# Attention values in the free quarter of the projection's PSUM bank, at the unit's end

## The chip, the cores and the metric

The kernel runs on one core of one Trainium2 chip. The metric is the device time of the program in microseconds; a run's time is compared with that of the kernel before. Engines are named as in the profile: PE is TensorE's matmul and PEld its weight load, DVE is VectorE, ACT is ScalarE, POOL is GpSimd, SP issues the transfers.

## The reference

One layer of retention, then one layer of differential attention, over 1024 tokens of width 1024. What matters here is the second layer, with 8 heads; each head has two query and key parts of 64 columns and values of 128 columns:

```python
kv = rmsnorm(x, kv_norm) @ w_kv            # keys (rotated) and values
proj = h @ w_in_b                          # queries (rotated) and gate
# for each head and each block of 128 queries, keys up to the block's end:
sc = einsum('bqhtd,bkhtd->bhtqk', q_i, kf) * scale
p = softmax(where(mask, sc, neg))          # for both parts t
w = p[:, :, 0] - lam * p[:, :, 1]
o = einsum('bhqk,bkhe->bqhe', w, vf)
o = rmsnorm(o, sub_norm_b) * (1 - lambda_init)
y = (o * silu(gate)) @ w_out_b
```

## The kernel before

All products of activations with weights are made three times, from a high and a low part of each operand (`mm3`, L95 to L100; the parts are made by `split`, L85 to L92, the high one by ScalarE, the low one by VectorE). The retention layer, its output projection and the gate of the second layer come first and aren't touched. The stage that is changed lies between about 949 and 1405 us.

In it a loop runs over 64 units, 8 heads times 8 token blocks of 128. A unit projects one token block for one head: eight slabs of 128 rows, three matmuls each, into 384 columns of one PSUM bank (`pq`: 256 columns of q and k, 128 of v). After the last slab `rotate_b` applies the rotary embedding: two products on VectorE out of the bank (L501, L502), their sum on GpSimd (L503), and the copy of v by ScalarE (L504). In the next unit `transpose_b` turns the 128 rows of q and k on TensorE (L512) and splits them (L87 on ScalarE, L88 on VectorE).

Between the slabs, two units behind (`LAG = 2`), the attention of one query block is done in pieces, which the generator `attend` hands out:

- `scores`: the two score products (L526; 6 matmuls for blocks 0 to 3, 12 for blocks 4 to 7), VectorE's mask and maximum (L532, L533), ScalarE's exponentials (L534), VectorE's combination of both softmaxes into one weight tile (L536 to L539).
- `turn`: the weight tile is transposed on TensorE, at most four blocks of 128 keys at a time (L551), and copied to wT by ScalarE (L552). Blocks 4 to 7 need two such pieces.
- `values`: the product of wT with v (L562; the trace has two instructions for each block of keys), the copy out of PSUM with a scale (L565), a sum of squares (L566), the power on GpSimd (L105 on VectorE, L106), the normed output (L568) and its store to `og2d` (L569).

In step j of `attend` the pieces are `scores` of block j, `values` of block j-2, and `turn` of block j-1; they run behind slabs 1, 3, 5 and 7. `transpose_b` runs behind slab 4.

PSUM has three groups of buffers: "g", two of one bank (the projection's `pq` among them), "s2", two of two banks (the scores), and "s", two of one bank. Before the change four things of a unit use "s": the transposes of q and k, both `turn` pieces, and the product of `values`.

`ahead` loads and splits the next head's weights (L90, L91), in the trace in the last unit of a head and the first of the next. After the loop `attend` still has steps to give; between their pieces the output projection runs (`out_prep`, which multiplies by the gate at L600 and transposes, and `out_gemm`), three groups of matmuls behind each piece.

The program is written in this order, but the framework lays out the order of every engine by its own estimate of when operands are ready, and sets all waits. It is seen in the trace: in most units TensorE's order is that of the program, in some, several projection matmuls stand ahead of a transpose.

Of the kernel before, what the change touches and what calls it, by code (L numbers as in the profile page):

```python
# [18 lines left out]
P = 128  # L19
# [16 lines left out]
def yoco_kernel(ctx: ExitStack, tc: tile.TileContext, a: dict):  # L36
# [16 lines left out]
    def sbuf(tag, shape, dt, nm):  # L53
        return sb.tile(shape, dt, name=f"{nm}_{next(uid)}", tag=tag, bufs=BUFS[tag])

    def xt(shape, nm, dt=F32R):
        return sbuf("x", shape, dt, nm)

    def wt(shape, nm, dt=F32R):
        return sbuf("w", shape, dt, nm)  # L60
# [7 lines left out]
    def kt(shape, nm, dt=F32):  # L68
        return sbuf("k", shape, dt, nm)

    def sm(n):
        return sbuf("m", [P, n], F32, "m")
# [3 lines left out]
    def ps(tag, n=512):  # L76
        return psum.tile([P, n], F32, name=f"p{tag}_{next(uid)}", tag=tag, bufs=PB[tag])
# [17 lines left out]
    def mm3(out, ops, first=True, last=True):  # L95
        n = 3 * len(ops)
        i = 0
        for lh, ll, rh, rl in ops:
            for l, r in ((lh, rh), (lh, rl), (ll, rh)):
                nc.tensor.matmul(out, l, r, start=(first and i == 0), stop=(last and i == n - 1))  # L100
                i += 1

    def rsqrt(out, in_, mul, add, n=1):
        t = sm(n)
        nc.vector.tensor_scalar(out=t, in0=in_, scalar1=mul, scalar2=add, op0=ALU.mult, op1=ALU.add)  # L105
        nc.gpsimd.tensor_tensor(out=out, in0=t, in1=mhalf[:, 0:n], op=ALU.pow)  # L106
# [166 lines left out]
    prev = None  # L273
    early = [ps("g"), ps("g")]
    gemm_qkv(list(enumerate(early)), w_next[0], range(NS))
    for i in range(H * NC):
        h, c = divmod(i, NC)
        if c == 0:
            wq, wg = w_next
        u = {"h": h, "c": c, "wg": wg, "pp": ps("s2", 1024)}  # L280
# [11 lines left out]
        prev = u  # L292
# [138 lines left out]
    def x2s(c, s):  # L431
        th, o = c // 4, (c % 4) * P
        return x2T[th][0][:, s, o : o + P], x2T[th][1][:, s, o : o + P]

    def gemm_piece(pq, w, c, s):
        mm3(pq, [(*x2s(c, s), w[s][:, 0, :], w[s][:, 1, :])], s == 0, s == NS - 1)
# [10 lines left out]
    def ahead(w, c, s):  # L447

        if s == 0 and 1 <= c <= 4:
            slab(w, c - 1)  # L450
        if c == NC - 1 and s < 4:
            slab(w, 4 + s)
# [21 lines left out]
    w_cur, w_next = w_next, []  # L474
    gate_unit(0, 0)
    fin1(NC - 1)
    for u in range(1, 2 * NC):
        if u == NC:
            w_cur, w_next = w_next, []
# [13 lines left out]
    def rotate_b(h, c, pq):  # L493

        qk, v = group(h, c)
        r = rot
        x4 = pq[:, 0:256].rearrange("p (x e d) -> p x e d", x=4, e=2)
        o4 = lambda t: t.rearrange("p (x e d) -> p x e d", x=4, e=2)
        cb = cosB[:, c, :].unsqueeze(1).unsqueeze(1).to_broadcast([P, 4, 2, 32])
        snb = ssinB[:, c].unsqueeze(1).to_broadcast([P, 4, 2, 32])  # L500
        nc.vector.tensor_tensor(out=o4(r[:, 0]), in0=x4, in1=cb, op=ALU.mult)  # L501
        nc.vector.tensor_tensor(out=o4(r[:, 1]), in0=x4[:, :, ::-1], in1=snb, op=ALU.mult)  # L502
        nc.gpsimd.tensor_tensor(out=r[:, 2], in0=r[:, 0], in1=r[:, 1], op=ALU.add)  # L503
        nc.scalar.activation(v[:, c % 4], pq[:, 256:384], AF.Copy)  # L504
        return h, c, r

    def transpose_b(h, c, r):
        qk, v = group(h, c)
        o = (c % 4) * P
        pt = ps("s", 256)  # L510
        for i in range(2):
            nc.tensor.transpose(pt[:, i * P : (i + 1) * P], r[:, 2, i * P : (i + 1) * P], ident)  # L512
        pv = pt.rearrange("p (x k) -> p x k", x=2)
        split(qk[:, :, 0, o : o + P], qk[:, :, 1, o : o + P], pv)

    def scores(u):
        h, b, nk = u["h"], u["b"], u["nk"]
        q, qs = groups[h, b // 4][0][:, 0], slice(b % 4 * P, b % 4 * P + P)
        sc = [ps("s2", 1024) for t in range(2)]
        for c0 in range(0, nk, 512):  # L520
            n = min(512, nk - c0)
            k = groups[h, c0 // 512][0][:, 1]
            for i, (ql, kl) in enumerate(((0, 0), (0, 1), (1, 0))):
                for t in range(2):
                    rows = slice(t * 64, t * 64 + 64)
                    nc.tensor.matmul(  # L526
                        sc[t][:, c0 : c0 + n], q[rows, ql, qs], k[rows, kl, 0:n], start=(i == 0), stop=(i == 2)
                    )
        nm, s_ = sm(2), sm(2)
        pr = [kt([P, D], f"pr{t}") for t in range(2)]  # L530
        for t in range(2):
            nc.vector.memset(sc[t][0:64, nk - 64 : nk], NEG)  # L532
            nc.vector.tensor_reduce(out=nm[:, t : t + 1], in_=sc[t][:, :nk], axis=AX.X, op=ALU.max, negate=True)  # L533
            nc.scalar.activation(pr[t][:, :nk], sc[t][:, :nk], AF.Exp, bias=nm[:, t : t + 1], accum_out=s_[:, t : t + 1])  # L534
        rc, cf = sm(2), sm(1)
        nc.vector.reciprocal(rc, s_)  # L536
        nc.vector.tensor_scalar(out=cf, in0=s_[:, 0:1], scalar1=rc[:, 1:2], scalar2=nlam, op0=ALU.mult, op1=ALU.mult)
        w = pr[0][:, :nk]
        nc.vector.scalar_tensor_tensor(out=w, in0=pr[1][:, :nk], scalar=cf, in1=w, op0=ALU.mult, op1=ALU.add)  # L539
        u.update(w=w, rc=rc)  # L540

    def turn(u, i):
        w = u["w"]
        if i == 0:
            u["wT"] = kt([P, D], "wT")
        k0, k1 = i * 512, min(u["nk"], i * 512 + 512)
        if k0 >= k1:
            return
        pt = ps("s")
        for k in range(k0, k1, P):  # L550
            nc.tensor.transpose(pt[:, k - k0 : k - k0 + P], w[:, k : k + P], ident)  # L551
        nc.scalar.activation(u["wT"][:, k0:k1], pt[:, : k1 - k0], AF.Copy)  # L552

    valued = set()

    def values(u):
        h, b, wT, rc = u["h"], u["b"], u["wT"], u["rc"]
        valued.add((h, b))
        po = ps("s", P)
        for kb in range(b + 1):  # L560
            v = groups[h, kb // 4][1]
            nc.tensor.matmul(po, wT[:, kb * P : (kb + 1) * P], v[:, kb % 4], start=(kb == 0), stop=(kb == b))  # L562
        o = sbuf("u", [P, 2, P], F32, "o")
        sq, r = sm(1), sm(1)
        nc.scalar.activation(o[:, 0], po, AF.Copy, scale=rc[:, 0:1])  # L565
        nc.scalar.activation(o[:, 1], o[:, 0], AF.Square, accum_out=sq)  # L566
        rsqrt(r, sq, 1.0 / P, EPS)
        nc.gpsimd.tensor_tensor(out=o[:, 1], in0=o[:, 0], in1=r.to_broadcast([P, P]), op=ALU.mult)  # L568
        nc.sync.dma_start(og2d[b * P : (b + 1) * P, h * P : (h + 1) * P], o[:, 1])  # L569

    def attend(blocks):

        blocks = [{"h": h, "b": b, "nk": (b + 1) * P} for h, b in blocks]
        a_, b_ = None, None
        for u in blocks + [None, None]:
            pieces = []
            if u:
                pieces.append(lambda: scores(u))
            if a_:
                pieces.append(lambda: values(a_))  # L580
            if b_:
                pieces.append(lambda: turn(b_, 0))
                if b_["nk"] > 512:
                    pieces.append(lambda: turn(b_, 1))
            yield pieces
            a_, b_ = b_, u


    wob = {}
# [1 line left out]
    def load_wob(f, hi, lo):  # L591
        wob[f] = load_wo(a["wob"], f, gsub, hi, lo)
# [46 lines left out]

    LAG = 2  # L640
    att = attend([(h, b) for h in range(H) for b in range(NC)])
    prev = None
    for i in range(H * NC):
        h, c = divmod(i, NC)
        if c == 0:
            w_cur, w_next = w_next, []
        pieces = next(att) if i >= LAG else []
        pq = ps("g", 384)
        for s in range(NS):
            gemm_piece(pq, w_cur, c, s)  # L650
            ahead(h + 3, c, s)
            if s == 4 and prev:
                transpose_b(*prev)
            if s % 2 == 1 and s // 2 < len(pieces):
                pieces[s // 2]()
        prev = rotate_b(h, c, pq)
        if h == H - 1:
            if c == 4:
                xw = [xt([P, 4, D], f"wob{hl}") for hl in range(2)]
            if 1 <= c <= 2:  # L660
                load_wob(c + 3, wt([P, D], "wobh"), wt([P, D], "wobl"))
            elif c >= 4:
                load_wob(c - 4, xw[0][:, c - 4], xw[1][:, c - 4])
# [4 lines left out]
    out_prep(0)  # L668
    og_ = outs()
    for step in att:  # L670
        for p in step:
            p()
            for _ in range(3):
                next(og_, None)
# [86 lines left out]
```

## Time and profile before

| | us |
|---|---|
| median of 3 runs | 1524.19 (1524.13 to 1524.55) |
| the profiled execution | 1519.59 |
| its span, first to last instruction | 1517.8 |
| TensorE busy in the span | 1480.0 |
| VectorE, ScalarE, GpSimd busy | 782.9, 626.3, 266.2 |

The granted TensorE clock was 0.997 of full speed over the span. A row of a timeline has the start, the duration of a run of like instructions, engine, line, operation, tiles, shapes, the count, and in brackets the idle time of the engine before it with what ended it. A row of waits has the engine and its line, whom it waited for, and the total, the count and the longest. A row of busy times by stretch has the stretch, its length, and the busy time (and count) of PE, PEld, DVE, ACT and POOL, the clock, the share of the transfer engines and GB/s.

### The profile page before, as it was taken

Reading aid. Unit: us, or ns where it says so; the run is one execution under the profiler, and the core shown is the slowest. Engines: PE = TensorE matmul, PEld = TensorE weight load, DVE = VectorE, ACT = ScalarE, POOL = GpSimd, SP = SyncE. Lnnn points to the kernel's source line nnn. Section 1 sums busy time; section 2 is a strip of 40 time slices with the busy share of each in tenths; the row PEclk is TensorE's granted clock in tenths of the full one; section 3 lists DMA queues with packets and bytes.
Section 4 is the critical chain, followed back from the end, with each engine's and each line's share of the span. In section 5 each row is a group of like instructions: output and inputs, shape, how many; then the busy total and the mean of one; then the engine's idle time right before and its main releaser. Section 6 shows DMA issues by size and latency. Waiting matters only on the chain.

```text
span 1517.8 us, 23752 instructions
## 1 busy us (share of the span) xinstructions
PE 1480.0 (98%) x8752; PEld 1296.0 (85%) x8752; DVE 782.9 (52%) x1968; ACT 626.3 (41%) x1591; POOL 266.2 (18%) x470
## 2 busy tenths in 40 slices
PE   6999999999999999999999999999999999999998
PEld 5888998888889888888877788988988988987786
DVE  5664645454545443541145511667567577577543
ACT  5542424242424232342244522456455466465421
POOL 1322222212222222200000000222222222222100
PEclk9999999999999999999999999999999999999999
DMA  7430302021211210353244522111011011023352
GB/s 272 146 111 15 97 15 88 22 82 31 60 53 47 62 62 30 98 191 104 98 153 167 190 95 71 34 47 52 10 51 51 11 51 51 12 92 115 116 174 84
DMA packets 70308, 125.63 MB, mean 83 GB/s; under 512 B 7600, under 2 KB 40752, under 8 KB 70192
## 3 DMA queue, kind: packets, MB, share of 16 engines
q1 hardware_dynamic: 70192, 124.11, 25.2%
q8 instruction: 69, 1.13, 0.3%
q14 instruction: 47, 0.39, 0.1%
HBM read 94.72 MB, written 29.36 MB: 82 GB/s over the span
## 4 chain that ended last, share of the span: by engine, by line
PE 80%; DVE 6%; DMA 5%; ACT 4%; issue 4%; POOL 1%; SPq 0%; DVEq 0%; POOLq 0%; ACTq 0%
PE pg L100 54%; PE ps L100 14%; PE ps L526 3%; PE ps L562 3%; PE ps L551 2%; DMA stg<-in_wa 1%; ACT pr L534 1%; DMA stw<-in_wa 1%; PE ps L313 1%; DVE wbh L91 1%; PE ps L234 1%; DMA og<-ogd 1%; PE ps L512 1%; DMA xr<-in_x 1%; DVE m L533 1%
## 5 line engine op out<-in xcount | busy, mean ns | idle before, releaser
L100 PE MATMUL pg<-wq,xT 128*128 128x512 f32 x1536 | 387.6, 402 | 8.8 <-ACT wq L90 7.1
L100 PEld LDWEIGHTS pg<-wq,xT 128*128 128x128 f32 x1536 | 281.5, 190 | 65.0 <-ACT wq L90 7.1
L100 PE MATMUL pg<-wbh,x2T 128*128 128x384 f32 x1536 | 334.6, 353 | 0.0
L100 PEld LDWEIGHTS pg<-wbh,x2T 128*128 128x128 f32 x1536 | 256.4, 189 | 13.0 <-issue 9.3
L106 POOL TENSOR_TENSOR m<-m,mhalf 128x1 f32<-128x1 f32 x152 | 83.3, 548 | 652.8 <-DVE m L105 591.2
L100 PE MATMUL ps<-wg,xT 128*128 128x256 f32 x1536 | 194.8, 283 | 0.0
L100 PEld LDWEIGHTS ps<-wg,xT 128*128 128x128 f32 x1536 | 189.1, 192 | 0.1
L534 ACT ACTIVATE pr<-ps,m 128x256 f32<-128x256 f32 (+7 forms) x128 | 94.0, 737 | 92.1 <-DVE m L533 92.1
L209 POOL TENSOR_TENSOR a<-a 128x256 f32<-128x256 f32 x64 | 48.1, 752 | 340.4 <-DVE a L208 324.9
L533 DVE TENSOR_REDUCE m<-ps 128x1 f32<-128x256 f32 (+7 forms) x128 | 91.1, 753 | 0.0
L100 PE MATMUL pg<-wbg,x2T 128*128 128x512 f32 x384 | 87.9, 390 | 0.8 <-DVE wbg L91 0.8
L90 ACT ACTIVATE r<-pg,tabA 128x256 fp32r<-128x256 f32 x64 | 30.1, 470 | 136.7 <-DVE a L208 136.2
L100 PEld LDWEIGHTS pg<-wbg,x2T 128*128 128x128 f32 x384 | 71.8, 188 | 16.0 <-DVE wbg L91 1.2
L100 PEld LDWEIGHTS ps<-r,r 128*128 128x128 f32 x528 | 72.1, 190 | 8.6 <-ACT r L236 2.6
L235 DVE TENSOR_TENSOR a<-ps,tabA 128x128 f32<-128x128 f32 x64 | 18.5, 289 | 116.5 <-PE ps L234 116.5
L100 PE MATMUL ps<-r,r 128*128 128x256 f32 x528 | 74.8, 283 | 2.4 <-ACT r L236 2.0
L562 PE MATMUL ps<-v,wT 128*128 128x128 f32 x576 | 74.7, 275 | 0.0
L562 PEld LDWEIGHTS ps<-v,wT 128*128 128x128 f32 x576 | 73.2, 191 | 0.7 <-DVE m L105 0.4
L503 POOL TENSOR_TENSOR tabB<-tabB 128x256 f32<-128x256 f32 x64 | 48.5, 758 | 127.9 <-DVE tabB L502 127.6
L207 DVE TENSOR_TENSOR a<-pg,tabA 128x256 f32<-128x256 f32 x64 | 27.0, 423 | 80.6 <-PE pg L100 80.5
L236 ACT ACTIVATE r<-a 128x128 fp32r<-128x128 f32 x64 | 19.8, 309 | 111.6 <-DVE a L235 111.5
L100 PE MATMUL pg<-wo,oh 128*128 128x512 f32 x192 | 59.9, 391 | 0.0
(142 smaller groups left out, 2344.0 us busy)
## 6 DMA issues: line engine op xcount, KB each, us to landing
stw<-in_wa SPq DMA_DIRECT2D x64, 256.0 KB, 3.0
stb<-in_wbh SPq DMA_DIRECT2D x64, 192.0 KB, 2.4
xr<-in_x SPq DMA_DIRECT2D x16, 512.0 KB, 4.2
stg<-in_wa SPq DMA_DIRECT2D x32, 256.0 KB, 3.3
ogd<-a SPq DMA_DIRECT2D x64, 128.0 KB, 1.9
sto<-in_woa SPq DMA_DIRECT2D x16, 512.0 KB, 4.8
og<-ogd SPq DMA_DIRECT2D x16, 512.0 KB, 5.0
y0d<-y SPq DMA_DIRECT2D x8, 512.0 KB, 3.2
```

The lines of the kernel that those rows point to most:

```text
L90: nc.scalar.activation(hi, src, AF.Copy, scale=scale)
L100: nc.tensor.matmul(out, l, r, start=(first and i == 0), stop=(last and i == n - 1))
L106: nc.gpsimd.tensor_tensor(out=out, in0=t, in1=mhalf[:, 0:n], op=ALU.pow)
L207: nc.vector.tensor_tensor(out=o4(t1), in0=q4, in1=cb, op=ALU.mult)
L209: nc.gpsimd.tensor_tensor(out=qk, in0=t1, in1=t2, op=ALU.add)
L236: nc.scalar.activation(ss[:, 0, :], sc, AF.Copy)
L503: nc.gpsimd.tensor_tensor(out=r[:, 2], in0=r[:, 0], in1=r[:, 1], op=ALU.add)
L526: nc.tensor.matmul(sc[t][:, c0 : c0 + n], q[rows, ql, qs], k[rows, kl, 0:n], start=(i == 0), stop=(i == 2))
L533: nc.vector.tensor_reduce(out=nm[:, t : t + 1], in_=sc[t][:, :nk], axis=AX.X, op=ALU.max, negate=True)
L534: nc.scalar.activation(pr[t][:, :nk], sc[t][:, :nk], AF.Exp, bias=nm[:, t : t + 1], accum_out=s_[:, t : t + 1])
L551: nc.tensor.transpose(pt[:, k - k0 : k - k0 + P], w[:, k : k + P], ident)
L562: nc.tensor.matmul(po, wT[:, kb * P : (kb + 1) * P], v[:, kb % 4], start=(kb == 0), stop=(kb == b))
```

## The change

`pq` takes a whole bank of 512 columns; the projection uses columns 0 to 383, and `values` writes its product to columns 384 to 511 once all eight slabs are done, ahead of `rotate_b`. `attend` is one step shorter: in step j it gives `scores` of block j, and `turn` and `values` of block j-1. The pieces have fixed slabs: `scores` behind slab 1, `turn` behind slabs 3 and 5 (5 and 7 before), `values` at the end. `transpose_b` moves from slab 4 to slab 2. In the steps after the loop `values` still takes a buffer of "s".

```diff
-    def values(u):
+    def values(u, pq=None):
         h, b, wT, rc = u["h"], u["b"], u["wT"], u["rc"]
         valued.add((h, b))
-        po = ps("s", P)
+        po = ps("s", P) if pq is None else pq[:, 384:512]
...
-        a_, b_ = None, None
-        for u in blocks + [None, None]:
-            pieces = []
+        old = None
+        for u in [{"h": h, "b": b, "nk": (b + 1) * P} for h, b in blocks] + [None]:
+            p = {}
             if u:
-                pieces.append(lambda: scores(u))
-            if a_:
-                pieces.append(lambda: values(a_))
-            if b_:
-                pieces.append(lambda: turn(b_, 0))
-                if b_["nk"] > 512:
-                    pieces.append(lambda: turn(b_, 1))
-            yield pieces
-            a_, b_ = b_, u
+                p[1] = lambda: scores(u)
+            if old:
+                p[3] = lambda: turn(old, 0)
+                if old["nk"] > 512:
+                    p[5] = lambda: turn(old, 1)
+                p["end"] = lambda *pq: values(old, *pq)
+            yield p
+            old = u
...
-        pieces = next(att) if i >= LAG else []
-        pq = ps("g", 384)
+        pieces = next(att) if i >= LAG else {}
+        pq = ps("g")
         for s in range(NS):
-            gemm_piece(pq, w_cur, c, s)
+            gemm_piece(pq[:, 0:384], w_cur, c, s)
             ahead(h + 3, c, s)
-            if s == 4 and prev:
+            if s == 2 and prev:
                 transpose_b(*prev)
-            if s % 2 == 1 and s // 2 < len(pieces):
-                pieces[s // 2]()
+            if s in pieces:
+                pieces[s]()
+        if "end" in pieces:
+            pieces["end"](pq)
         prev = rotate_b(h, c, pq)
...
     for step in att:
-        for p in step:
+        for p in step.values():
             p()
             for _ in range(3):
                 next(og_, None)
```

More of the change, by code (lines that the diff above doesn't have):

```diff
@@ L571, in attend @@
     def attend(blocks):
-        blocks = [{"h": h, "b": b, "nk": (b + 1) * P} for h, b in blocks]
-        a_, b_ = None, None
-        for u in blocks + [None, None]:
-            pieces = []
+        old = None
+        for u in [{"h": h, "b": b, "nk": (b + 1) * P} for h, b in blocks] + [None]:
+            p = {}
             if u:
-                pieces.append(lambda: scores(u))
-            if a_:
-                pieces.append(lambda: values(a_))
-            if b_:
-                pieces.append(lambda: turn(b_, 0))
-                if b_["nk"] > 512:
-                    pieces.append(lambda: turn(b_, 1))
-            yield pieces
-            a_, b_ = b_, u
+                p[1] = lambda: scores(u)
[6 more added lines that the diff above has]
+            old = u
     wob = {}
```

## The prediction

> **What bounds the kernel now.** I read the page's first part first, then the busy times of the attention stage (949 to 1405 us) alone, then TensorE's waits in that stretch, then two units of it in order of time.
>
> ```profile
> PE 1480.0 (98%) x8752; PEld 1296.0 (85%) x8752; DVE 782.9 (52%) x1968; ACT 626.3 (41%) x1591; POOL 266.2 (18%) x470
> ...
> PE 80%; DVE 6%; DMA 5%; ACT 4%; issue 4%; POOL 1%; SPq 0%; DVEq 0%; POOLq 0%; ACTq 0%
> ```
>
> ```profile
> 949.00:1405.00 456.00, 447.67 (x2995) 401.77 (x2994) 300.84 (x807) 253.45 (x762) 105.02 (x184) 1.00 0.16 48
> ```
>
> TensorE is the bound, in the whole span and in the stage that is changed: 447.67 of 456 us busy. The change neither adds nor removes a matmul, a copy or a byte, so it can only move the few microseconds in which TensorE waits. Those are (TensorE's two rows for that window, then the first of the weight load: total us, times, longest):
>
> ```profile
> PE ps L551 <- ACT o L565: 5.9, 9, 1.5
> PE ps L512 <- POOL tabB L503: 2.2, 2, 1.9
> ...
> PEld ps L551 <- ACT o L565: 10.6, 17, 1.8
> ```
>
> The reader should see that one wait dominates: the transposes of the weights (L551, `turn`) wait for ScalarE's copy of the attention output out of PSUM (L565, in `values`). They share the two buffers of tag "s". This is the unit in which it happens once per head (scores of block 6):
>
> ```profile
> 1107.42 0.97 PE L526 MATMUL ps<-qk,qk 64*128 64x512 f32 x6
> ...
> 1108.84 1.33 PE L100 MATMUL pg<-wbh,x2T 128*128 128x384 f32 x6
> ...
> 1110.01 1.28 PE L562 MATMUL ps<-v,wT 128*128 128x128 f32 x10
> ...
> 1110.47 2.09 DVE L533 TENSOR_REDUCE m<-ps 128x1 f32<-128x896 f32 x2
> ...
> 1111.65 1.01 ACT L534 ACTIVATE pr<-ps,m 128x896 f32<-128x896 f32 x1 [1.29 <-DVE m L533]
> 1111.66 0.38 PE L512 MATMUL ps<-ident,tabB 128*128 128x128 f32 x2
> 1111.79 0.77 PE L100 MATMUL pg<-wbh,x2T 128*128 128x384 f32 x3
> ...
> 1112.65 0.36 ACT L565 ACTIVATE o<-ps,m 128x128 f32<-128x128 f32 x1
> 1112.73 0.48 DVE L91 SCALAR_TENSOR_TENSOR wbh<-stb,gains,wbh 128x256 fp32r<-128x256 f32 x1
> ...
> 1113.06 0.66 PE L551 MATMUL ps<-ident,pr 128*128 128x128 f32 x4 [0.50 <-ACT o L565]
> ...
> 1114.42 0.42 DVE L88 TENSOR_TENSOR qk<-ps,qk 128x256 fp32r<-128x256 f32 x1
> ...
> 1114.75 1.14 DVE L539 SCALAR_TENSOR_TENSOR pr<-pr,m,pr 128x896 f32<-128x896 f32 x1
> ```
>
> VectorE is late here (weight splits, L91, sit among its work), so the first exponential is late, and the output copy queued behind it on ScalarE ends at 1113.01, when TensorE has already run dry.
>
> **The change part by part.** The sum is made on the profiled execution (span 1517.8 us, 1519.59 us in all); the median of the runs shown is 1524.19, so I add the difference to that.
>
> *A. Output copy no longer holds an "s" buffer.* The value product goes to columns 384 to 511 of the projection's bank, so `turn` no longer waits for L565. Nine waits of TensorE, 5.9 us by its own row; 10.6 us by the weight load's row, which also counts time in which earlier matmuls were still draining. Bounds -5.9 and -10.6; I take the middle, **-8 us**. What comes next there: the exponentials, the copies of wT and the output product are then waited for by nothing sooner than the unit's end.
>
> *B. Transposes of the weights two slabs sooner.* Their input, the combined weights, was finished a unit earlier, so the first (`turn` 0) waits for nothing. The second reuses the "s" buffer of the rotated q and k (L512), and so waits for VectorE's L88 on them. In the unit above: the scores now start 1.28 later (the ten output matmuls that stood at 1110.01 now stand before them), at 1108.70. Steps from the rows here and in the next fence: scores 1.42 (1107.42 to 1108.84), three projection matmuls 0.61 (1127.71 to 1128.32), the q/k transposes 0.13 (1111.66 to 1111.79), again three 0.62 (1128.45 to 1129.07), four transposes 0.35 (1129.07 to 1129.42), six projection matmuls 1.15 (1129.42 to 1130.57): the second `turn` is reached at 1112.98. L88 could run right after the two reductions, ending at 1112.56 + 0.42 = 1112.98 (no wait), or behind the last weight split (L91), ending at 1113.21 + 0.42 = 1113.63 (0.6 us). Eight heads: 0 to +5 us. The build lays out each engine's order by its own estimate of what is ready (L88 stands ahead of L539 above, though the program has it behind the whole score block), so I take half, **+2.4 us**.
>
> *C. Rotation behind the value product.* This is the added wait. VectorE's rotation (L501, L502) reads the bank that TensorE now writes last and ScalarE reads first. Rows of a light unit (scores of block 0):
>
> ```profile
> 1123.35 1.32 PE L100 MATMUL pg<-wbh,x2T 128*128 128x384 f32 x6
> ...
> 1124.60 0.55 PE L526 MATMUL ps<-qk 64*128 64x128 f32 x6
> ...
> 1125.08 1.31 PE L100 MATMUL pg<-wbh,x2T 128*128 128x384 f32 x6
> 1125.20 0.73 POOL L503 TENSOR_TENSOR tabB<-tabB 128x256 f32<-128x256 f32 x1
> ...
> 1126.23 1.72 PE L562 MATMUL ps<-v,wT 128*128 128x128 f32 x14
> ...
> 1127.71 0.77 PE L100 MATMUL pg<-wbh,x2T 128*128 128x384 f32 x3
> 1128.04 0.37 ACT L565 ACTIVATE o<-ps,m 128x128 f32<-128x128 f32 x1 [1.53 <-issue]
> ...
> 1128.32 0.38 PE L512 MATMUL ps<-ident,tabB 128*128 128x128 f32 x2
> 1128.45 0.77 PE L100 MATMUL pg<-wbh,x2T 128*128 128x384 f32 x3
> ...
> 1129.07 0.60 PE L551 MATMUL ps<-ident,pr 128*128 128x128 f32 x4
> 1129.11 0.55 POOL L106 TENSOR_TENSOR m<-m,mhalf 128x1 f32<-128x1 f32 x1 [3.17 <-DVE m L105]
> ...
> 1129.42 1.31 PE L100 MATMUL pg<-wbh,x2T 128*128 128x384 f32 x6
> ...
> 1129.73 0.40 POOL L568 TENSOR_TENSOR o<-o,m 128x128 f32<-128x128 f32 x1
> ...
> 1130.57 0.60 PE L551 MATMUL ps<-ident,pr 128*128 128x128 f32 x4
> 1130.84 0.42 DVE L501 TENSOR_TENSOR tabB<-pg,tabB 128x256 f32<-128x256 f32 x1 [1.26 <-PE pg L100]
> ...
> 1131.18 0.41 DVE L502 TENSOR_TENSOR tabB<-pg,tabB 128x256 f32<-128x256 f32 x1
> ...
> 1131.69 0.27 ACT L504 ACTIVATE v<-pg 128x128 f32<-128x128 f32 x1
> 1131.73 0.73 POOL L503 TENSOR_TENSOR tabB<-tabB 128x256 f32<-128x256 f32 x1 [1.60 <-DVE tabB L502]
> ```
>
> Today GpSimd's sum (L503) ends at 1125.93 and its transpose starts at 1128.32: 2.4 us of slack. That L504 starts only when L502 has ended (1131.59) shows that two engines' reads of one bank are put one after the other; so the new order is value product, L565, L501, L502, L503, transposes. From the end of the product: L565 starts 0.09 later (1127.95 to 1128.04) and takes 0.37; 0.1 to L501; 0.34 to L502; 0.55 to L503; 0.73: ready at 2.18. TensorE meanwhile: the next projection matmul starts 0.24 before the product's end (1127.71 against 1127.95), six take 1.25 (1123.35 to 1124.60), scores of block 0 take 0.48 (1124.60 to 1125.08), three matmuls 0.61: transposes reached at 2.10. So the slack falls from 2.4 us to about nothing where the next scores are short (blocks 0 to 3, four units in eight), and stays positive where they are long (block 6 takes 1.42 for them, 0.94 more).
>
> Lower bound 0. The upper bound is GpSimd's order: the output's norm (L106, L568) is ready 1.07 after L565 starts (1128.04 to 1129.11) and ends at 1130.13, 2.18 after the product. If both stand before L503, the transposes are ready near 3.0, 0.9 late: for four units and eight heads at most +29 us. If only L106 (0.55) does, it is 0.4 late at block 0 and less after. The layout would move projection matmuls in front of a transpose that it sees to be late, so only what it misjudges is lost: I take 0.1 us in four units of eight heads, **+3 us**, near the lower bound, because the plain sum above gives 0.08.
>
> The Trainium skill (PSUM — Partial Sum Buffer, PSUM bank collisions raise a hardware error) says that any two of TensorE, ScalarE and VectorE must be kept apart on one bank and quadrant, reads against reads included, whatever columns they touch. By that the free columns of a bank aren't free for another engine, and the full chain above applies; if only overlapping columns counted, VectorE would start 0.56 us sooner and term C would be nothing. The gap from L502's end to L504's start agrees with the rule.
>
> *D. End of the stage.* The rows:
>
> ```profile
> 1387.74 1.23 DVE L600 TENSOR_TENSOR og<-og,g 128x1024 f32<-128x1024 f32 x1 [2.25 <-DMA g<-gd]
> ...
> 1391.23 0.66 PE L551 MATMUL ps<-ident,pr 128*128 128x128 f32 x4 [1.51 <-ACT o L565]
> ...
> 1404.69 0.44 PE L512 MATMUL ps<-ident,tabB 128*128 128x128 f32 x2 [1.95 <-POOL tabB L503]
> ```
>
> Two of the nine waits of A are from L600, which holds VectorE until a load lands. That stays: output blocks come a unit earlier, L600 moves with them, and delays rotation or reductions instead. I give back **+2 us** (0 to +4). The wait of 1.95 us after the last unit remains about as it is: ±1, taken as **-0.7** since one unit's value product (ten matmuls, 1.28) now lies before it. One step fewer in the last loop only regroups the output matmuls, which run back to back after it: 0.
>
> *Taken at nothing.* SP: the 64 stores of the output wait for L568 at another place; a store at a unit's end can hold back weight loads issued behind it by up to those 2.2 us, hidden while the splits (L91) end before the slab's matmuls. ScalarE and VectorE do the same work. The 512-wide bank replaces a 384-wide one in the same two buffers; it is freed by L504, later by the product and L565 (about 2 us), a unit before it is needed (8.6 us: the scores at 1107.42 and at 1124.60 are two units apart). First and last matmuls after each switch are the same in number.
>
> Sum: -8 + 2.4 + 3 + 2 - 0.7 = -1.3 us, so 1522.9 us: no change that can be told. A difference under 0.2% (3.0 us) is about what a measurement of this kernel can't tell from none.
>
> **Rivals.**
> 1. *The gain stays* (faster). The layout fills every new wait with projection matmuls: A without B and C: -8 + 2 - 0.7 = -6.7, 1517.5 us. For it: it already keeps all but nine such waits away. Against it: the slack of 2.4 us that hid its errors is spent.
> 2. *The rotation chain is exposed* (slower). GpSimd takes the norm before the sum, or ScalarE comes late to L565. From 0.25 us per light unit (32 of them, 8 us instead of 3) the total passes +3; at 0.4, with B in full: -8 + 5 + 12.8 + 2 - 0.7 = +11, 1535 us. For it: in the unit shown L568 comes before L503. Against it: L503's inputs come 1.45 after the product (0.09 + 0.37 + 0.1 + 0.34 + 0.55), before L106 and L568 would both be done (2.18).
> 3. *The wait only changes its name.* VectorE's lateness in block 6 is not touched, and `turn` 1 waits on L88 for as long as `turn` 0 did on L565: A returns as B and D: 1524 us.
>
> **How the numbers follow.** The forecast with rival 3, both within 0.2% (1521.1 to 1527.2): 0.42. Rival 1 and what lies between: 0.30. Rival 2: 0.28. The likeliest alone, with two of its terms at their ends, spans 1518 to 1528. The range reaches to rival 1 with A nearly at its bound (-10.6 + 2 - 0.7, 1514.9) and to rival 2 (1535), leaving out 0.2: 1515.5 to 1534. Faster 0.30, same 0.42, slower 0.28.
>
> **What would show it.** A right: the waits of L551 on L565 are gone. B: waits of L551 on L88 in the units with scores of block 6, up to 0.6 us. C: L501 starts about 0.1 after L565's end in every unit; waits of L512 on L503 appear, 0.1 us each, in the units with scores of blocks 0 to 3; if they are 0.4 or more, rival 2. D: L600 still ahead of a wait of about 1 to 2 us. The forecast is wrong if TensorE's order changes so that a group that I counted on is no longer there to cover a chain.

## The result, and the profile after

The changed kernel is slower: 1533.96 us (median of 5 runs) against 1524.13 us, a ratio of 1.0064 with a 95% interval of 1.0049 to 1.0078. A second measurement gave 1.0070 (1.0052 to 1.0089). The profiled executions took 1528.53 and 1519.59 us.

TensorE's busy time hardly moved (1480.0 us before), and its share of the changed stage fell. The page's first line and the row of that stretch, of the changed kernel:

```profile
PE 1482.7 (97%) x8752; PEld 1295.5 (85%) x8752; DVE 782.4 (51%) x1968; ACT 633.0 (41%) x1591; POOL 269.9 (18%) x470
```

```profile
949.00:1405.00 456.00, 443.17 (x2955) 395.15 (x2954) 290.78 (x788) 255.44 (x749) 105.59 (x182) 1.00 0.14 44
```

447.67 us of work in 456 have become 443.17, with 40 matmuls fewer in the same stretch: the same work takes longer. TensorE's waits in 949 to 1414 us (matmul rows, then rows of the weight load):

```profile
PE ps L512 <- POOL tabB L503: 12.9, 17, 2.4
PE ps L551 <- DVE qk L88: 1.7, 7, 0.2
PE ps L526 <- DVE qk L88: 0.9, 1, 0.9
PE pg L563 <- ACT wT L552: 0.6, 1, 0.6
...
PEld ps L512 <- POOL tabB L503: 20.0, 24, 2.7
...
PEld ps L551 <- DVE qk L88: 4.3, 8, 0.6
PEld pg L563 <- ACT wT L552: 2.1, 8, 0.9
```

The old wait, L551 on the output copy (10.6 us of the weight load's idle time), is gone. In its place stands the one that was to be 3 us in all: the transposes of q and k (L512) wait for GpSimd's sum (L503), 2.9 us of weight-load idle time before and 20.0 now. (The value product's line is 563 here, its copy 566, its norm 569.)

A head is the time between the first score matmul of block 0 in two consecutive heads. Before, the one at 1124.60 is followed by this one, 58.28 us later:

```profile
1182.88 0.55 PE L526 MATMUL ps<-qk 64*128 64x128 f32 x6
```

After:

```profile
1125.98 0.55 PE L526 MATMUL ps<-qk 64*128 64x128 f32 x6
...
1185.28 0.55 PE L526 MATMUL ps<-qk 64*128 64x128 f32 x6
```

59.30 us, and 59.35 as a mean of four heads in a row (59.30 to 59.39): about 1.07 us more in each of eight heads, 8.6 us. From the loop's first projection matmul to its last it took 456.5 us before, 465.4 after and 464.8 in the second measurement's profile, so most of the loss lies in the loop. Behind it, from the end of the last projection matmul to that of the last output matmul, it took 110.0 us before and 113.2 after (114.8 in the second). That this comes from the shared bank isn't shown: among the runs below, two that share the bank took 109.5 and 110.0 us there, and two that share none 112.9 and 114.2.

In a steady head two units lose nearly all of it, the one with scores of block 0 about 0.5 us and the one with scores of block 6 about 0.9. The unit with scores of block 0, the counterpart of the light unit shown before, from its two pieces of weight transposes (L551) on:

```profile
1120.40 0.60 PE L551 MATMUL ps<-ident,pr 128*128 128x128 f32 x4
...
1120.76 1.83 PE L100 MATMUL pg<-wbh,x2T 128*128 128x384 f32 x9
...
1122.42 0.49 PE L551 MATMUL ps<-ident,pr 128*128 128x128 f32 x3
...
1122.67 1.11 PE L100 MATMUL pg<-wbh,x2T 128*128 128x384 f32 x5
...
1123.62 1.72 PE L563 MATMUL pg<-v,wT 128*128 128x128 f32 x14
1125.10 0.95 PE L100 MATMUL pg<-wbh,x2T 128*128 128x384 f32 x4
1125.43 0.37 ACT L566 ACTIVATE o<-pg,m 128x128 f32<-128x128 f32 x1 [1.65 <-issue]
...
1125.90 0.42 DVE L501 TENSOR_TENSOR tabB<-pg,tabB 128x256 f32<-128x256 f32 x1 [1.16 <-ACT o L566]
1125.98 0.55 PE L526 MATMUL ps<-qk 64*128 64x128 f32 x6
1126.24 0.42 DVE L502 TENSOR_TENSOR tabB<-pg,tabB 128x256 f32<-128x256 f32 x1
1126.46 0.79 PE L100 MATMUL pg<-wbh,x2T 128*128 128x384 f32 x3
...
1126.80 0.73 POOL L503 TENSOR_TENSOR tabB<-tabB 128x256 f32<-128x256 f32 x1 [6.97 <-DVE m L105]
...
1127.59 0.44 PE L512 MATMUL ps<-ident,tabB 128*128 128x128 f32 x2 [0.34 <-POOL tabB L503]
```

The chain is the forecast one to 0.02 us: product's end 1125.34, copy, rotation 0.10 behind the copy, sum's end 1127.53, 2.19 later (forecast 2.18). What differs is the cover, the work that TensorE still has between the product and the transposes: four projection matmuls stand behind the product, not six. The rows show where they went. The second piece of weight transposes stands nine projection matmuls behind the first, where the program has six, and the product five behind that, two of them from the next unit. Presumably the layout expected L551 to wait for L88 and the product for wT, and moved matmuls there. The unit with scores of block 6:

```profile
1106.73 1.38 PE L563 MATMUL pg<-v,wT 128*128 128x128 f32 x10
...
1107.87 0.60 PE L100 MATMUL pg<-wbh,x2T 128*128 128x384 f32 x2
...
1108.20 0.37 ACT L566 ACTIVATE o<-pg,m 128x128 f32<-128x128 f32 x1
...
1108.43 0.48 DVE L91 SCALAR_TENSOR_TENSOR wbh<-stb,gains,wbh 128x256 fp32r<-128x256 f32 x1
...
1108.83 0.42 DVE L501 TENSOR_TENSOR tabB<-pg,tabB 128x256 f32<-128x256 f32 x1
...
1109.41 0.55 POOL L106 TENSOR_TENSOR m<-m,mhalf 128x1 f32<-128x1 f32 x1 [6.67 <-DVE m L105]
...
1110.04 0.54 POOL L569 TENSOR_TENSOR o<-o,m 128x128 f32<-128x128 f32 x1
...
1110.54 0.77 POOL L503 TENSOR_TENSOR tabB<-tabB 128x256 f32<-128x256 f32 x1
...
1111.36 0.44 PE L512 MATMUL ps<-ident,tabB 128*128 128x128 f32 x2 [0.75 <-POOL tabB L503]
```

Here only two projection matmuls follow the product before the scores, VectorE is held by a weight split, and GpSimd takes the norm (L106, L569) before the sum: 3.2 us from the product's end (1108.11) to the sum's end (1111.31).

The following sums are worked out from the traces: TensorE's start-to-start times ahead of a group, beyond the 0.17 to 0.18 us that one projection matmul takes, over 949 to 1400 us.

| us lost ahead of | before | changed | own buffer | late transposes | copy after rotation | copy twice |
|---|---|---|---|---|---|---|
| q/k transposes (L512) | 0.5 | 13.7 | 2.2 | 0.8 | 3.4 | 12.4 |
| weight transposes (L551) | 9.2 | 3.0 | 8.0 | 9.1 | 10.3 | 8.4 |
| value product | 0.1 | 0.9 | 0.1 | 0.8 | 0.1 | 0.1 |

Of the 13.7 us, 11.0 lie in the units with scores of blocks 6 and 0. In the last head 2.1 lie ahead of L512 in the units of blocks 2 and 3, and 0.4 in the loop's first unit. The loop as a whole, first to last projection matmul, took 456.5, 465.4, 457.0, 458.7, 462.2 and 471.3 us in the order of the columns.

### The profile page after: what moved, and what is told of

Read it like the earlier page. It is cut to its first block, busy times and chain, and to the rows that moved or that the text cites. A ratio compares the mean times of both kernels' runs of the same rounds, so it can differ in the third digit from the quotient of the medians.

```text
span 1526.8 us, 23684 instructions
## 1 busy us (share of the span) xinstructions
PE 1482.7 (97%) x8752; PEld 1295.5 (85%) x8752; DVE 782.4 (51%) x1968; ACT 633.0 (41%) x1591; POOL 269.9 (18%) x470
## 5 line engine op out<-in xcount | busy, mean ns | idle before, releaser
L106 POOL TENSOR_TENSOR m<-m,mhalf 128x1 f32<-128x1 f32 x152 | 86.6, 570 | 406.1 <-DVE m L105 406.0
L503 POOL TENSOR_TENSOR tabB<-tabB 128x256 f32<-128x256 f32 x64 | 47.7, 745 | 382.1 <-DVE m L105 286.4
L235 DVE TENSOR_TENSOR a<-ps,tabA 128x128 f32<-128x128 f32 x64 | 18.5, 290 | 114.2 <-PE ps L234 114.1
L501 DVE TENSOR_TENSOR tabB<-pg,tabB 128x256 f32<-128x256 f32 x64 | 27.1, 424 | 86.2 <-ACT o L566 83.2
L563 PE MATMUL pg<-v,wT 128*128 128x128 f32 x534 | 70.3, 276 | 0.6 <-ACT wT L552 0.6
L563 PEld LDWEIGHTS pg<-v,wT 128*128 128x128 f32 x534 | 67.5, 191 | 2.2 <-ACT wT L552 2.1
L236 ACT ACTIVATE r<-a 128x128 fp32r<-128x128 f32 x64 | 19.8, 309 | 109.5 <-DVE a L235 109.4
```

Source lines behind the costliest of these rows:

```text
L235: nc.vector.tensor_tensor(out=sc, in0=pS, in1=mask, op=ALU.mult)
L236: nc.scalar.activation(ss[:, 0, :], sc, AF.Copy)
```

## The experiments

### The product in a buffer of its own

```diff
-        po = ps("s", P) if pq is None else pq[:, 384:512]
+        po = ps("s", P)
```

> The changed kernel, but the value product at the unit's end takes a buffer of tag s again, not the projection's bank. Theory (shared bank): VectorE's rotation L501 starts about 0.1 us after the last projection matmul instead of after the value product and ScalarE's copy, GpSimd's sum is there 1 to 2 us sooner, and the waits of the q/k transposes L512 on L503 (20 us of the weight load's idle time in the changed kernel) fall to under 5 us. One head falls from 59.35 us to about 58.4; some of it may return as waits of the weight transposes L551 on the output copy, since they share tag s again. Time 1525 to 1528 against 1524 before and 1534 changed. Rival (transposes too early): the transposes of q and k at slab 2 are reached before the rotation is done whatever bank the product uses; then L512 still waits over 10 us and the time stays at 1531 to 1535.

Measured 0.9991 of the kernel before (0.9982 to 1.0000), 1520.65 us; a head 58.48. The waits of its TensorE:

```profile
PE ps L551 <- DVE qk L88: 5.8, 7, 1.0
PE ps L512 <- POOL tabB L503: 2.9, 3, 1.6
...
PEld ps L551 <- DVE qk L88: 10.1, 14, 1.3
...
PEld ps L512 <- POOL tabB L503: 3.9, 3, 1.9
```

The loss is gone with this one line, though the transposes still stand at slab 2. TensorE's matmuls stand in the same order as in the changed kernel through the first six heads, so the cover is as short here. The unit with scores of block 0:

```profile
1129.93 0.95 PE L100 MATMUL pg<-wbh,x2T 128*128 128x384 f32 x4
...
1130.47 0.73 POOL L503 TENSOR_TENSOR tabB<-tabB 128x256 f32<-128x256 f32 x1 [6.84 <-DVE tabB L502]
...
1131.91 0.38 PE L512 MATMUL ps<-ident,tabB 128*128 128x128 f32 x2
```

Four projection matmuls again, but the sum ends at 1131.20, 0.71 us before the transposes start. In the next unit the rotation (L501) starts under the product of 16 matmuls, 1.7 us before its end:

```profile
1135.64 1.95 PE L563 MATMUL ps<-v,wT 128*128 128x128 f32 x16
1135.91 0.42 DVE L501 TENSOR_TENSOR tabB<-pg,tabB 128x256 f32<-128x256 f32 x1 [2.10 <-PE pg L100]
```

It was faster than expected (1525 to 1528); the end behind the loop took 109.6 us here. The 2.2 us that L512 still loses lie in the last head and the first unit, so the shared bank's part of the 13.7 is 11.5. Of it 5.0 come back ahead of L551 (3.0 and 8.0 in the table), and the three sums together fall from 17.6 to 10.3. What remains is the once-per-head wait, now L551 on L88, where the output copy was expected.

### Late transposes, early transposes, and both undone

```diff
-            if s == 2 and prev:
+            if s == 4 and prev:
```

> The changed kernel with the transposes of q and k back behind slab 4; the value product stays in the projection's bank. Both theories: they come two slabs and a turn later (about 1.5 us), which is more than the longest wait of 0.9 us, so L512 no longer waits and a head falls to about 58.0 to 58.5 us. What tells apart: by the shared-bank theory the late rotation is harmless here, 1523 to 1527; if something else of the new order costs the time (the value product at the end waiting for wT, the tail), it stays above 1529.

1.0025 (1.0012 to 1.0037), 1527.21 us, a head mostly 58.75. L512's loss fell to 0.8 us, L551's rose to 9.1. The head missed what was expected (58.0 to 58.5). About 60% of the slowdown in time goes when the transposes come late, with the bank still shared.

The same edit the other way, on the kernel before:

> The kernel before with one edit, the transposes of q and k behind slab 2 instead of 4. Theory (shared bank): GpSimd's sum had 1.85 to 3.7 us of slack before its transposes in a steady head; the move takes three projection matmuls and the value product out of it (0.9 to 2.6 us), so slack stays positive nearly everywhere and the time is 1522 to 1526. Rival (transposes too early): waits of L512 on L503 appear as in the changed kernel, one per unit with short scores, and the time is 1529 or more.

1.0023 (1.0013 to 1.0033): 3.5 us slower, a head 58.5 to 58.6, L512 losing 5.0 us. The time is 1526.38 us, just above what the shared-bank theory allowed and below its rival's 1529; waits of L512 do appear, 0.3 us a head in the unit with scores of block 0. So early transposes cost something by themselves in the order of before, less than half of the loss. In the order of the change, with the product at the unit's end, slab 2 and slab 4 can't be told apart once the bank isn't shared, as the next run shows.

The own buffer together with slab 4:

> The changed kernel with both suspects undone: the value product in a buffer of tag s and the transposes of q and k behind slab 4. What is left of the change is the earlier weight transposes and the pipeline one step shorter. Theory (all of the loss is the rotation behind the shared bank): as the own buffer alone, a head at 58.2 to 58.6 us, 1519 to 1524. Rival (the late transposes gain something of their own): below 58.0 and 1517 or less.

0.9990 (0.9977 to 1.0002), a head 58.6. No difference from the own buffer alone (0.9991). The earlier weight transposes and the shorter pipeline, all that is left of the change here, are worth nothing that can be told.

### The chain shorter and longer by one copy

`values` is split, and its copy, square, norm and store are issued behind `rotate_b`:

```diff
         prev = rotate_b(h, c, pq)
+        if "copy" in pieces:
+            pieces["copy"]()
```

> The changed kernel, with ScalarE's copy of the output product issued behind the rotation instead of ahead of it; the product stays in the shared bank. Theory (the rotation waits for the whole chain product, copy): the rotation starts 0.1 after the product's end instead of 0.56 after; the waits of L512 on L503 (20.0 us of the weight load's idle time) fall by about 0.45 us in each of the two units per head that lose most (scores of blocks 6 and 0), to 8 to 12 us, and a head falls from 59.35 to 58.5 to 58.9 us; time 1526 to 1531. Rival (what delays the rotation is the product itself, not the copy): L512 waits as before and the time stays at 1533 to 1535.

1.0021 (1.0008 to 1.0034), 1526.95 us; a head 59.14. L512 lost 3.4 us instead of 13.7, and its idle time on the weight load fell to 5.2:

```profile
PEld ps L551 <- DVE qk L88: 13.4, 20, 1.1
...
PEld ps L512 <- POOL tabB L503: 5.2, 12, 1.4
```

The time came as expected, but the head did not fall to 58.5 to 58.9: most of the transposes' gain came back as waits of L551 on L88.

```diff
+        if pq is not None:
+            nc.scalar.activation(o[:, 1], po, AF.Copy, scale=rc[:, 0:1])
         nc.scalar.activation(o[:, 0], po, AF.Copy, scale=rc[:, 0:1])
```

> The changed kernel with ScalarE's copy out of the shared bank done twice (0.4 us more between product and rotation, the rest alike). Theory (the rotation chain has no slack left in five units of a head): each of the units with scores of blocks 0, 1, 2, 3 and 6 loses 0.3 to 0.4 us more, a head rises from 59.35 to 60.7 to 61.5 us, the time to 1544 to 1552. Rival (only the two units with a rearranged order, blocks 6 and 0, are at their limit): a head rises by 0.8 us, the time to 1538 to 1542. If the layout covers it with other matmuls, it stays at 1533 to 1536.

1.0086 (1.0066 to 1.0105), 1537.11 us; a head 60.33, 0.98 more. From one score group to the next, blocks 0, 1 and 2 took 0.26, 0.25 and 0.21 us more, block 3 only 0.02, block 5 0.24, block 6 none. So the chain is at its limit in the three units with the shortest scores, and the layout or other waits take up the rest. The head lies between what the two theories gave (60.7 to 61.5, and 0.8 more), the time just below the rival's 1538. In time alone the run can't be told from the changed kernel: its interval overlaps both of that kernel's.

### The once-per-head wait: can it be had without the loss?

The order of before, the product in the free quarter of the bank of the unit before:

```diff
-        po = ps("s", P)
+        po = held[0][:, 384:512] if held else ps("s", P)
...
         prev = rotate_b(h, c, pq)
+        held[:] = [pq]
```

> The kernel before with its order and depth kept (weight transposes at slabs 5 and 7, q/k transposes at 4, two steps deep), but the value product behind slab 3 goes to the free quarter of the bank of the unit before, which the rotation has read by then. By term A alone: L551 no longer waits for the output copy (10.6 us of the weight load's idle time before), and the rotation waits for nothing new: 1515 to 1521. By the rival that the wait only changes its name (VectorE is as late as before, and L551 then waits for L88 or for wT): 1523 to 1526.

0.9997 (0.9985 to 1.0009): the third rival. The rotation waits for nothing new, L551 no longer waits for the output copy (L567 here), and a head takes 58.30. Its unit with scores of block 6:

```profile
1111.63 2.09 DVE L533 TENSOR_REDUCE m<-ps 128x1 f32<-128x896 f32 x2
...
1115.05 0.39 ACT L87 ACTIVATE qk<-ps 128x256 fp32r<-128x256 f32 x1
...
1115.31 0.61 ACT L552 ACTIVATE wT<-ps 128x512 f32<-128x512 f32 x1
...
1115.59 0.41 DVE L88 TENSOR_TENSOR qk<-ps,qk 128x256 fp32r<-128x256 f32 x1
...
1115.98 0.44 PE L551 MATMUL ps<-ident,pr 128*128 128x128 f32 x2 [0.73 <-ACT wT L552]
```

The first weight transposes go through, and the second wait for ScalarE's copy of the first (L552, done at 1115.92), which stands behind the exponentials; VectorE's L88 ends only at 1116.00, when they have started. 0.9 us are lost; before, 0.66 ahead of the first and 0.20 ahead of the second.

The pieces reordered (scores 1, first weight transposes 3, product 5, second 7), with the bank of the unit before, and with tag "s":

> The order of the kernel before with the value product in the free quarter of the bank of the unit before, and the pieces rearranged: scores behind slab 1, the first weight transposes behind 3, the q/k transposes 4, the value product 5, the second weight transposes 7. Theory (the once-per-head wait belongs to whatever reuses an s buffer too soon while VectorE is late): the second weight transposes now come a value product and two slabs after the q/k transposes (2.5 us or more instead of 1.9), so the wait of 0.9 us per head is gone: a head at 57.6 to 57.9 us against 58.3, time 1515 to 1519 against 1522 to 1524 before. Rival (VectorE's lateness always lands on TensorE): a head stays at 58.2 or more, another wait takes its place, 1521 to 1526.

> The same rearranged order on the kernel before, with the value product in tag s as it was: no bank is shared. Theory: the first weight transposes no longer come behind the output copy on ScalarE, so the old wait (10.6 us of the weight load's idle time) goes without any bank sharing; the value product now takes the buffer of the first weight transposes and may wait for their copy. A head at 57.6 to 58.0 us, time 1515 to 1520. Rival (another wait takes its place): 1521 to 1526.

1.0001 (0.9988 to 1.0013) and 0.9998 (0.9984 to 1.0011); heads of 58.15 and 58.5. In the first, projection matmuls wait for the bank that the product still holds (L567, its copy); in the second the product waits for its buffer:

```profile
PE pg L100 <- ACT o L567: 2.8, 8, 0.9
```

```profile
PE ps L562 <- DVE qk L88: 5.9, 7, 1.0
PE ps L562 <- ACT wT L552: 2.2, 2, 1.9
```

In both another wait takes its place, as the rival said, and the times can't be told from before. The head of the first, 58.15, lies just below the rival's 58.2, far from the theory's 57.6 to 57.9.

### VectorE relieved at the head's end

```diff
-        split(w[:, 0, P:], w[:, 1, P:], st[:, P:], g_kv[:, s : s + 1])
+        nc.scalar.activation(w[:, 0, P:], st[:, P:], AF.Copy, scale=g_kv[:, s : s + 1])
+        nc.gpsimd.tensor_tensor(out=w[:, 1, P:], in0=w[:, 0, P:], in1=w[:, 0, P:], op=ALU.subtract)
```

> The kernel before, with part of the work left out: the low part of the k and v weights of each head isn't computed on VectorE; GpSimd writes zeros there (0.75 us, eight times a head). VectorE is spared 0.47 us a slab, 3.8 us a head, all of it in the two units where a head's weights are split. Theory (the once-per-head wait of L551 on the output copy comes from VectorE's lateness there): the wait goes, a head falls from 58.28 to 57.5 to 57.8 us, the time by 4 to 6 us. Rival (the wait comes from the order of the pieces alone): a head stays within 0.2 us of 58.28 and the time within 2 us of before.

0.9996 (0.9983 to 1.0009), a head 58.1: a miss, 0.16 us instead of 0.5 to 0.8, and within what the rival allowed. The step from block 6 to block 7 fell from 8.81 to 8.25 us, that from 5 to 6 rose from 7.47 to 7.90. The traces show both halves: ahead of the weight transposes the unit with scores of block 6 loses 0.3 us instead of 0.9, with TensorE's order as before, and the unit of block 5 loses 0.45 instead of 0.06, now waiting for L88. So VectorE's lateness is a cause of the wait in that unit, but relieving VectorE moved most of the wait instead of removing it.

> The changed kernel with the same work left out (low part of the k and v weights, zeros by GpSimd instead). Theory (two losses: late VectorE at the head's end in the unit with scores of block 6, about 0.9 us, and in that of block 5, about 0.4; the bare chain product, copy, rotation, sum in that of block 0, 0.5): the first two go or shrink, the last stays; a head falls from 59.35 to 58.2 to 58.6 us, still 0.5 to 1 us above the kernel before with the same work left out. Rival (the whole loss is the bare chain): a head stays above 59.

1.0031 (1.0017 to 1.0045), 1527.06 us; heads of 58.4 in the fourth to sixth, up to 59.45 in the others. The step from block 6 fell from 9.13 to 8.63 (means of five heads), from block 5 from 8.11 to 7.80; the step from block 0 stayed (8.32 and 8.33). Ahead of L512 the unit of block 6 lost nothing in the first six heads, though only two projection matmuls stand behind its product here too; the unit of block 0 lost 0.5 us in each head, as in the changed kernel. So the loss has two sources: the bare chain in the light unit, and the same chain lengthened by late VectorE work at a head's end. How much of that was VectorE's and how much GpSimd's order isn't separated: here GpSimd had work of its own added.

### The changed kernel again

> The changed kernel unchanged, on the same chip as the three others. Both theories: 1.005 to 1.008 of the kernel before; a head at 59.3 to 59.4 us. It tells how much of the spread between runs lies in the stages ahead of the loop, whose instructions stand in the same order in both kernels: the loop's head should repeat within 0.05 us, the end of the gate stage by several us.

1.0070 (1.0052 to 1.0089); a head 59.33 to 59.43.

## Why the prediction was wrong

**What held.** A: the loss ahead of L551 fell from 9.2 to 3.0 us, 6.2 less; A and B together were forecast at -5.6. The wait changed from L565 to L88, as said, but in the unit with scores of block 5, one before the one named, at 0.4 us. The rule of the Trainium skill on one bank (PSUM — Partial Sum Buffer, PSUM bank collisions raise a hardware error) agrees with the traces: in the changed kernel L501 starts 0.10 us after the copy's end, though their columns are apart, and under the product once the bank isn't shared. The prediction's 0.56 us for the latter counted only from the product's end. The chain's length was right, 2.19 us against 2.18.

**The step that failed is the size of C.** Forecast 3 us, measured 13.2 (0.5 to 13.7 ahead of L512); 11.5 of the 13.7 go when the bank isn't shared. It failed in three places:
- The cover. I counted six projection matmuls behind the product. The layout put two (block 0) or four (block 6) of them in front of it. Cover of 0.35 and 0.7 us was spent on other waits. The text named this as what would make it wrong, and gave it no price.
- The unit with scores of block 6 was left out, with 0.86 us of slack by its long scores. It lost most, 0.9 us: its cover was 0.7 short, and the sum came 1.0 later than the plain chain, by a weight split ahead of L501 and GpSimd's norm ahead of the sum, the order that I had given to rival 2 and to short scores only.
- The 0.1 us that I took for what the layout misjudges was too small for block 0: 0.5 us was lost in each head, identically.

B as such came out near its price, 3.0 us ahead of L551 against 2.4. But the second weight transposes were also placed three or four matmuls late, and that came out of C's cover.

**D.** The wait after the last unit was to shrink by 0.7. It grew, from 1.9 to 2.4 us, and scores there waited 0.9 us for L88, 1.2 in the second measurement; that L88 stands behind L600, which still waits for its load (1.78 us), as D said. The end behind the loop took 3.2 us more in the profile, where the two parts of D made +1.3. Since that length changes by as much between runs without following the bank, its cause stays open.

**The rivals.** Rival 2's direction and its mechanism in the wide sense, the rotation chain exposed, came true, and its 11 us is close to the 9.8 measured. That closeness is partly luck: it charged 0.4 us to 32 light units (12.8 us), while the loss was 0.5 in the light units of block 0, little in those of blocks 1 to 3, and 0.9 in those of block 6, which aren't light; and in block 0 neither GpSimd's order nor a late ScalarE took part. The sum as measured in the loop is A and B -6.2, the product's own wait 0.8, C 13.2, about +8 (8.6 by the heads). Rival 3 is what happens when the product stays out of the bank that its unit's rotation reads: that is the own buffer and the previous bank. Rival 1's case, a gain that stays, was found in no order that was tried.

**What stays open.** The profiles' heads and the times agree only roughly: with the copy after the rotation the heads add 7 us and the time 3.2 (1.2 to 5.2). Why the layout placed the matmuls as it did isn't seen in a trace, only where it placed them.

## What to carry to other kernels

In this kernel a free corner of a PSUM bank was free only for the engine that held the bank: what was put there joined the chain of everything that still had to read the rest. Before moving work to a place with slack, count the slack in the order that the build will lay out, not in the order of the program, because the filler that covers one wait is taken from the cover of the next. A wait on an engine that is late need not go away with the buffer it showed up on: here the once-per-head wait kept its size of about 0.9 us when the buffer was given, and ended on another instruction.

## What the runs showed of the hardware

The stages ahead of the loop have TensorE's instructions in the same order in both kernels, and yet the gate stage's last matmul ended between 941.2 us (the changed kernel) and 950.1 us (the copy after the rotation) after the span's start; the same code of the changed kernel gave 941.2 and 946.2 in two runs. Its second to fifth heads repeated within 0.1 us. The end behind the loop took between 109.5 and 114.8 us in the fourteen profiles, 113.2 and 114.8 with the same code. A difference of a few microseconds between two profiles is read from the stage, not from the span.
